# A gated DeltaNet layer whose convolution is done piece by piece behind each projection, with the scan traced closer together

## The chip, the cores and the metric

The kernel runs on one core of a Trainium2 chip. Its time is the device time of one execution in microseconds (us), from the first instruction to the last. Engines are named as in the profile: PE is the matrix engine (PEld its loading of weights), DVE the vector engine, ACT the scalar engine, POOL the GpSimd engine, SP the engine that issues most transfers. Every engine takes its instructions in the order of its own queue. An instruction waits on semaphores for what it needs of the other engines and of the DMA queues, and what stands behind it in its queue waits with it.

## What is computed

One step of a hybrid decoder with two layers, on 1,024 prompt tokens and 8 sequences of 8 new tokens (1,088 columns in all), with a width of 1,024. The first layer is a gated DeltaNet with 8 heads of 128, then a feed-forward layer; the second is a windowed attention mixture, then a feed-forward layer. The change touches the DeltaNet alone:

```python
proj = h @ w_in                                            # per head: q, k, v, gate of 128 columns each
xh = concat([conv_hist, proj[..., :A_CONV_DIM]], axis=1)    # 3 earlier rows ahead of the tokens
c = silu(causal_depthwise_conv(xh, conv_w))                 # 4 taps per column
q = l2_normalize(c_q) * A_DK ** -0.5; k = l2_normalize(c_k); v = c_v
...
def step(s, xs):                                            # one chunk of tokens of one head
    w_c, u_c, attn_c, q_c, k_c, ge_c = xs
    u = u_c - w_c @ s
    o = q_c @ s + attn_c @ u
    s = ge_c * s + k_c.T @ u
    return s, o
s_fin, o = lax.scan(step, s0, (w_mat, u_base, attn, q_dec, k_dec, g_end))
o = rms_norm(o, o_gain) * silu(gate)
```

Before the scan, each chunk needs the inverse of a triangular system of its decayed key products (`w_mat`, `u_base`).

## The kernel before

All values are float32; a product with weights is made as three passes of a split into a high and a low part (`h_hi`, `h_lo` and `w[0]`, `w[1]`), so one block of 128 output columns is 72 matmuls (L764).

A head goes through three stages, and three heads are worked on at a time. In round i of `gdn`, `gdn_scan` works on head i - 2, `gdn_prep` on head i - 1 and `gdn_dense` on head i; some gate projections fill the late rounds. `merge` traces the stages side by side: each yields the share of itself that it has just traced, and the one with the smallest sum goes next. From that tracing a scheduler makes the order of each engine's queue. So the numbers behind `yield` set how far apart the steps of a stage stand, in units of the others' work.

`gdn_dense` projects the three blocks (q, k, v) of a head, each in three chunks of tokens, 384, 352 and 352 wide (the last has 288 prompt and 64 new tokens). ACT copies a chunk from PSUM to the tile `xr` (L801, L803), which starts with 3 earlier rows. When all chunks of a block are there, `yc` is made from `xr`: ACT multiplies all 1,112 columns with the first tap (L809) and DVE adds the other three taps (L811). ACT's Silu follows (L813, L815), and the block goes to DRAM (L816). `xr` and `yc` have one buffer each; POOL clears the first 3 columns of the next `xr` at L795 and copies the last rows out at L805 and L806. Weights are loaded and split by `wtile`: ACT makes the high part (L142), POOL or DVE the low part (L145).

`gdn_prep` loads the head's q, k and v, transposes them on PE (L934), takes the keys' decay into `kdec` on DVE (L958) with their squares on ACT (L941), and makes the products of keys with keys and queries (L987). DVE builds the decay tile `aT` (L963), ACT its exponential (L965). `rq` is the queries' inverse norm (POOL's power at L1008 between DVE's L1007 and L1009). A row elimination on small blocks (L1020 to L1022, 15 steps) gives `dc`, from which DVE makes Dx (L1032), E (L1059) and its transpose F (L1048). NZ and NZ2 are two tiles that POOL clears (L1038) and ACT fills with parts of N (L1040, L1042); the first product of the inverse (L1054) takes NZ and F. NZ shares its buffer with the values and the queries.

`gdn_scan` goes through 8 chunks: p1 (L1166), r on DVE (L1168), p2 (L1173), u on ACT (L1175), p3 (L1178), the new state S on DVE (L1181), and the output from two products (L1185, L1187) with ACT's L1189 and DVE's L1190. The new tokens' step (`decode`, with POOL's `kqm` at L1121) is traced between the chunks. Behind the loop ACT squares the nine tiles of the output (L1203), POOL makes the factor (the norm chain, L1204 to L1208) and multiplies the output `vs` with it (L1211); PE transposes that (L1219) and ACT copies it out (L1225).

Of the kernel before, what the change touches and what calls it, by code (L numbers as in the profile page):

```python
# [22 lines left out]
P = 128  # L23
# [17 lines left out]
def tok(tt):  # L41
    return (tt * P, P) if tt < 8 else (SP, SD)


def merge(*threads):
    """Traces generators side by side: each yields the share of itself that it has just traced."""
    done = [[0.0, i, t] for i, t in enumerate(threads)]
    while done:
        done.sort()
        try:  # L50
            done[0][0] += next(done[0][2])
        except StopIteration:
            done.pop(0)


def staged(items, *stages):
    """Traces stage s of an item beside stage s + 1 of the item before; each takes the item and its last stage's result."""
# [8 lines left out]
def stream(*stages):  # L66
    """push(item) traces the first stage of an item, the second of the last item, and so on; None drains."""
# [12 lines left out]
class Net:  # L80
# [13 lines left out]
    def banks(self, **tags):  # L94
        """PSUM for the phase that follows: how many of the eight banks go around under each tag."""
# [6 lines left out]
    def weights(self, es, rb, wb, side=None):  # L102
        """Rotating [128, 1024] tiles for the enclosing phase: rb as they arrive, wb pairs of split weights."""
# [23 lines left out]
    def wtile(self, view, shape, gain=None, eng=None):  # L127
        """view: DRAM AP whose shape is `shape` ([128, a, b] or [128, n]); n <= 1024 columns."""
# [19 lines left out]
    def rstd(self, ss, p, n=D):  # L148
        """(ss / n + eps) ** -0.5 on a [p, c] tile."""
# [10 lines left out]
    def h_tiles(self):  # L160
        """High and low parts of a normed input, feature-major."""
        return tuple(self.hpool.tile([P, KD, T], F32R, tag=n, name=n) for n in ("h_hi", "h_lo"))

    def scale(self, tt, x, grow, xn=None):
        """Normed tokens x [p, 1024], times the gain if there is one."""
# [14 lines left out]
    def flipped(self, x, hi, lo, bank):  # L180
        """x [p, n * 128] feature-major, split, to hi and lo [128, n, p]."""
# [11 lines left out]
    def turn(self, tt, xn, h, bank):  # L193
        """xn feature-major, split, to its columns of h."""
# [10 lines left out]
    def residual(self, tt, y, xin, xout, grow, store=None):  # L205
        """x' = x + rms(y) * gain in place in y [p, 1024]; x' goes to xout in DRAM. A quarter of the columns is made without VectorE."""
# [16 lines left out]
    def fast_pool(self, es):  # L223
        """Space for the operands of fast products (see ffn_in), for the next chunk of the tokens; those that are free first lie together."""
# [12 lines left out]
    def stow(self, tt, x, grow):  # L237
        """Normed tokens x beside those of the other half that they go with."""
# [6 lines left out]
    def mate(self, tt, bank, tmp):  # L245
        """The seven moving operands of the fast product (see ffn_in) for tile tt of the second half and its mate of the first,
        one at a time; tmp() is [128, 1024]."""
# [1599 lines left out]
```

## Time and profile before

| | us |
|---|---|
| median of 3 runs | 3467.95 |
| lowest of the runs | 3462.15 |
| profiled execution: span, which is its own time | 3468.3 |
| PE busy in the span | 3104.6 (90%) |
| DVE busy | 2265.7 (65%) |
| ACT busy | 1556.7 (45%) |
| POOL busy | 1435.4 (41%) |

A row of the waits names the engine that waited, the line of the waiting instruction and, behind the arrow, the one that it waited for. In a timeline a row that ends with [idle before <- releaser] was preceded by idle time of that engine. The granted clock of PE (PEclk) is a share of its full speed.

### The profile page before, as it was taken

To read this page: it belongs to the slowest core of one execution; us is meant where nothing else is said; L and a number is where in the kernel's file an instruction comes from. 1 tells how busy PE (TensorE), PEld (TensorE's weight loads), DVE (VectorE), ACT (ScalarE), POOL (GpSimd) and SP (SyncE) were. 2 spreads that over 40 slices of the span, in tenths; PEclk is the share of its full clock that TensorE was granted. 3 is DMA by queue.
4 is the path that set the end of the run, shared out by engine and by line. 5 is a ranking of instruction groups with operands and counts; after the bars stand their busy time and mean duration, and the time that the engine had idled before them with its cause. 6 is when DMAs were issued, how large, how long until landed. Compare 5 with 4: busy or idle time off the path is not lost.

```text
span 3468.3 us, 53879 instructions
## 1 busy us (share of the span) xinstructions
PE 3104.6 (90%) x19768; PEld 2838.5 (82%) x19768; DVE 2265.7 (65%) x4705; ACT 1556.7 (45%) x3779; POOL 1435.4 (41%) x1368
## 2 busy tenths in 40 slices
PE   7899999999899999898899787978498999998996
PEld 7888888887799999776698787867276999997774
DVE  5677777625655555789767676767346655556888
ACT  5455554434433332533567676766134333334433
POOL 3333333343444443778421222221114344445877
PEclk8999999999999999999899998989789999999998
DMA  4223333344222221420531122213343122223213
GB/s 139 90 97 109 109 101 95 113 159 134 98 75 75 75 75 64 157 94 26 187 84 46 53 66 60 59 56 94 107 156 123 52 75 75 75 75 148 91 63 109
DMA packets 255588, 324.53 MB, mean 94 GB/s; under 512 B 33282, under 2 KB 204914, under 8 KB 255324
## 3 DMA queue, kind: packets, MB, share of 16 engines
q1 hardware_dynamic: 247324, 288.98, 26.1%
q0 software_dynamic: 7856, 31.56, 2.3%
q8 instruction: 156, 2.56, 0.3%
q14 instruction: 108, 0.88, 0.1%
q10 hardware_dynamic: 144, 0.56, 0.0%
HBM read 240.49 MB, written 80.55 MB: 93 GB/s over the span
## 4 chain that ended last, share of the span: by engine, by line
PE 56%; DVE 15%; DMA 8%; POOL 8%; ACT 6%; issue 4%; SPq 2%; POOLq 0%; DVEq 0%; ACTq 0%
PE mm L355 26%; PE mm L394 6%; PE mm L764 5%; PE mm L567 4%; DMA f<-fr 4%; PE mm L1344 2%; PE B L1054 2%; DVE og L1482 2%; SPq L1546 2%; ACT s L1435 2%; PE mm L1289 1%; DVE yc L811 1%; DVE qs L1355 1%; DVE wa L380 1%; PE A L987 1%
## 5 line engine op out<-in xcount | busy, mean ns | idle before, releaser
L394 PE MATMUL mm<-wa,ga 128*128 128x512 f32 x1872 | 474.8, 411 | 63.5 <-DVE wa L380 22.6
L394 PEld LDWEIGHTS mm<-wa,ga 128*128 128x128 f32 x1872 | 366.8, 198 | 165.2 <-DVE wa L380 32.8
L764 PE MATMUL mm<-h_hi,w 128*128 128x352 f32 (+1 forms) x1536 | 444.6, 348 | 10.5 <-ACT xr L801 8.2
L1344 PE MATMUL mm<-h_hi,w 128*128 128x352 f32 (+1 forms) x1152 | 374.3, 354 | 0.1
L764 PEld LDWEIGHTS mm<-h_hi,w 128*128 128x128 f32 x1536 | 283.5, 193 | 22.3 <-ACT xr L801 9.1
L323 POOL TENSOR_TENSOR wide<-wide,v 128x288 f32<-128x288 f32 (+1 forms) x176 | 162.3, 937 | 245.4 <-DVE v L322 245.4
L764 PE MATMUL mm<-h_lo,w 128*128 128x352 f32 (+1 forms) x768 | 260.0, 339 | 0.0
L304 DVE TENSOR_TENSOR s<-w,s 128x512 fp32r<-128x512 f32 x132 | 164.8, 1250 | 129.4 <-ACT s L303 129.2
L303 ACT ACTIVATE s<-t 128x512 fp32r<-128x512 f32 x176 | 111.0, 631 | 288.0 <-PE mm L355 275.0
L294 POOL TENSOR_TENSOR t<-w 128x512 f32<-128x512 f32 x88 | 114.6, 1304 | 299.0 <-issue 170.3
L1344 PEld LDWEIGHTS mm<-h_hi,w 128*128 128x128 f32 x1152 | 222.0, 197 | 0.6 <-PE mm L1344 0.3
L1435 ACT ACTIVATE s<-s,stat 128x128 f32<-128x128 f32 (+1 forms) x384 | 168.9, 441 | 106.4 <-DVE stat L1433 105.0
L1344 PE MATMUL mm<-h_lo,w 128*128 128x352 f32 (+1 forms) x576 | 194.3, 337 | 0.0
L567 PE MATMUL mm<-mw_hi,o_hl 128*128 128x512 f32 x544 | 176.4, 400 | 7.5 <-DVE o_hl L556 3.9
L1547 POOL TENSOR_TENSOR og<-og,f 128x512 f32<-128x512 f32 x42 | 53.7, 1278 | 285.1 <-DMA f<-fr 285.1
L1448 PE MATMUL tr<-ident,s 128*128 128x128 f32 x560 | 98.8, 285 | 72.1 <-DVE pl L1452 70.9
L145 POOL TENSOR_TENSOR w<-raw,w 128x1024 fp32r<-128x1024 f32 x38 | 100.6, 2649 | 146.4 <-ACT w L142 124.7
L304 DVE TENSOR_TENSOR s<-t,s 128x512 fp32r<-128x512 f32 x176 | 131.6, 749 | 39.7 <-ACT s L303 39.4
L355 PE MATMUL mm<-b0h,s 128*128 128x256 f32 (+1 forms) x704 | 144.8, 293 | 12.2 <-ACT s L303 9.6
L1452 DVE TENSOR_TENSOR pl<-tr,ph 128x256 fp32r<-128x256 f32 (+1 forms) x192 | 103.9, 544 | 78.1 <-ACT ph L1451 77.4
L811 DVE SCALAR_TENSOR_TENSOR yc<-xr,convw,yc 128x1112 f32<-128x1112 f32 x72 | 115.5, 1604 | 54.5 <-ACT yc L809 54.4
L764 PEld LDWEIGHTS mm<-h_lo,w 128*128 128x128 f32 x768 | 149.0, 194 | 1.9 <-issue 0.9
(477 smaller groups left out, 9559.6 us busy)
## 6 DMA issues: line engine op xcount, KB each, us to landing
w<-in_ffn_w_in_dram SPq DMA_DIRECT2D x88, 512.0 KB
gd<-wide POOLq DMA_DIRECT2D x22, 1088.0 KB, 4.9
graw<-gd SPq DMA_DIRECT2D x44, 544.0 KB
wraw<-in_ffn_w_out_dram SPq DMA_DIRECT2D x44, 512.0 KB
raw<-in_a_w_in_dram SPq DMA_DIRECT2D x32, 512.0 KB
qkv<-f SPq DMA_DIRECT2D x24, 544.0 KB
xo<-x SPq DMA_DIRECT2D x24, 512.0 KB
raw<-in_b_w_q_dram SPq DMA_DIRECT2D x24, 512.0 KB
```

Of the source, the lines that this page charges most:

```text
L294: op(t, x, y)
L303: nc.scalar.activation(out[j][:, 0], x, AF.Copy)
L304: nc.vector.tensor_sub(out[j][:, 1], x, out[j][:, 0])
L323: nc.gpsimd.tensor_tensor(out, out, v, op=ALU.mult)
L355: nc.tensor.matmul(ps[:, :HC[c][1]], u, v, start=z == 0, stop=z == 11)
L394: nc.tensor.matmul(ps, a, b, start=i == 0, stop=i == len(seq) - 1)
L567: nc.tensor.matmul(ps, a, b[:, k], start=k == 0 and i == 0, stop=k == KD - 1 and i == len(seq) - 1)
L764: nc.tensor.matmul(ps[:, :n], a[:, k, :], b[:, k, n0:n0 + n], start=i_ == 0, stop=i_ == 23)
L811: nc.vector.scalar_tensor_tensor(yc, xr[:, j:j + CW], w(j), yc, op0=ALU.mult, op1=ALU.add)
L1344: nc.tensor.matmul(ps[:, :n], a[:, k, :], b[:, k, n0:n0 + n], start=i == 0, stop=i == 23)
L1435: nc.scalar.activation(s[:, a, :n], s[:, a, :n], AF.Exp, bias=m, scale=-1.0, accum_out=stat[:, 1, a, b:b + 1])
L1452: nc.vector.tensor_sub(pl[:, :nk], pt[:, :nk], ph[:, :nk])
```

## The change

The convolution moves into the loop over the chunks of a block. As soon as a chunk has been copied to `xr`, ACT multiplies its columns with the first tap and DVE adds the other three; `yc` is taken at the start of the block. Per block that is 3 instructions on ACT where there was 1, and 9 on DVE where there were 3, of 384, 352 and 376 columns. In the scan, the square of chunk c - 1 is traced at step c, the last two behind the loop, and the yields of the scan's steps become smaller, those behind the norm larger. The docstrings are gone too, so lines shift: L811 becomes L810, L809 becomes L808, L813 L815, L958 L960, L987 L989, L1008 L1010, L1038 L1040, L1040 L1042, L1054 L1056, L1121 L1123, L1187 L1198, L1203 L1171, L1204 to L1208 L1211 to L1215, L1211 L1218 and L1219 L1226.

```diff
@@ gdn_dense
             nc.vector.tensor_copy(xd[:, :, 0:3], hist[:, tl].rearrange("p (b j) -> p b j", j=3))
+            yc = dp.tile([P, XW], F32, name="yc")[:, :CW]
+            w = lambda j: cv[:, j, tl:tl + 1]
             for y in self.gdn_proj(tl * P, h, w_in):
...
                     if n0 + n > SP:
                         nc.scalar.activation(xd[:, :, 3:], ps[:, a1 - n0:n].rearrange("p (b l) -> p b l", l=DL), AF.Copy)
+                        a1 = CW
+                    yy = yc[:, n0:a1]
+                    nc.scalar.activation(yy, xr[:, n0:a1], AF.Copy, scale=w(0))
+                    for j in range(1, 4):
+                        nc.vector.scalar_tensor_tensor(yy, xr[:, j + n0:j + a1], w(j), yy, op0=ALU.mult, op1=ALU.add)
                 yield 1 / 72
...
-            yc = dp.tile([P, XW], F32, name="yc")[:, :CW]
-            w = lambda j: cv[:, j, tl:tl + 1]
-            nc.scalar.activation(yc, xr[:, 0:CW], AF.Copy, scale=w(0))
-            for j in range(1, 4):
-                nc.vector.scalar_tensor_tensor(yc, xr[:, j:j + CW], w(j), yc, op0=ALU.mult, op1=ALU.add)
@@ gdn_scan
         dec = decode()
+        half = self.mhalf[:, :NT]
+        ss, f = small("ss_o"), small("f_o")
+        nc.gpsimd.memset(ss, 1.0)
+
+        def squares(c0, c1):
+            for c in range(c0, c1):
+                n = tok(c)[1]
+                j = rtile("junk")
+                nc.scalar.activation(j[:n], o[:n, c], AF.Square, accum_out=ss[:n, c:c + 1])
...
-                yield 0.02
+                yield 0.015
                 next(dec, None)
                 yield 0.01
...
-            yield 0.03
+            yield 0.02
...
-            yield 0.03
+            if c:
+                squares(c - 1, c)
+            yield 0.02
         nc.sync.dma_start(delta_p[hd], S)
         for _ in dec:
             pass
-        half = self.mhalf[:, :NT]
-        ss, f = small("ss_o"), small("f_o")
-        nc.gpsimd.memset(ss, 1.0)
-        for c in range(NT):
-            n = tok(c)[1]
-            j = rtile("junk")
-            nc.scalar.activation(j[:n], o[:n, c], AF.Square, accum_out=ss[:n, c:c + 1])
+        squares(7, 9)
...
-        yield 0.1
+        yield 0.15
         for s, n in parts:
             nc.gpsimd.tensor_tensor(o[:n, s], o[:n, s], bc(f, s, n), op=ALU.mult)
-        yield 0.1
+        yield 0.2
```

The queues have, in the whole program, 156 more rows on DVE (4,166 to 4,322; the listing counts some runs of like instructions as one row) and 70 more on ACT (2,540 to 2,610), 12 of them loads of ACT's function tables (23 to 35). Only the DeltaNet heads differ; from the mixer behind them to the end the order is the same on all engines. On PE, a steady head of before has 48 projections between the scan's last product (L1187) and the norm transposes (L1219), which stand directly ahead of the first product of the inverse (L1054). Now there are 78 (and five transposes of the values) ahead of the norm transposes (L1226), and six more between these and L1056. The scan's last product stands at 36.6 of a head's 62.8 units of the listing's PE work where it stood at 43.4.

Three places of a steady head follow, each before and now. On POOL, behind the scan of a steady head (ss_o and f_o are the norm chain, vs the output, kqm the new tokens' products of the next head), the queue was:

```order
L1038 MEMSET NZ 128x1024
L805 COPY last<-xr 128x3
L806 COPY last<-xr 128x24
L145 TENSOR_TENSOR w<-raw,w 128x1024
L976 MEMSET nc 64x16
L1204 TENSOR_TENSOR ss_o<-ss_o,rq 128x9
L1205 TENSOR_TENSOR ss_o<-ss_o,rq 128x9
L1206 TENSOR_SCALAR ss_o<-ss_o 128x9
L1207 TENSOR_TENSOR f_o<-ss_o,mhalf 128x9
L1208 TENSOR_TENSOR f_o<-f_o,rq 128x9
L1199 MEMSET ss_o 128x9
L1211 TENSOR_TENSOR vs<-vs,f_o 128x1024
```
and is now:

```order
L1010 TENSOR_TENSOR rq<-nq,mhalf 128x9
L953 MEMSET nq 128x9
L1211 TENSOR_TENSOR ss_o<-ss_o,rq 128x9
L1212 TENSOR_TENSOR ss_o<-ss_o,rq 128x9
L1213 TENSOR_SCALAR ss_o<-ss_o 128x9
L1214 TENSOR_TENSOR f_o<-ss_o,mhalf 128x9
L1215 TENSOR_TENSOR f_o<-f_o,rq 128x9
L1165 MEMSET ss_o 128x9
L1218 TENSOR_TENSOR vs<-vs,f_o 128x1024
L1218 TENSOR_TENSOR vs<-vs,f_o 64x128
L1123 TENSOR_TENSOR kqm<-qT_5871,Q_514 128x4x64
L1040 MEMSET NZ 128x1024
```
The clearing of NZ stood ahead of the weights' split and the norm chain; it stands behind the chain, the product and kqm, and the weights' split behind both. The power for rq is now directly ahead of the chain.

On ACT, at the end of the scan of a steady head (L1203 and L1171 are the squares, L801 and L803 the evacuations of a projection, u and t the scan's own), the queue was:

```order
L1203 ACTIVATE junk,ss_o<-vs 128x128
L1040 ACTIVATE NZ<-N 32x8x32 x4
L1175 ACTIVATE u<-C,bcol 128x128
L801 ACTIVATE xr<-mm 128x288
L803 ACTIVATE xr<-mm 128x8x8
L142 ACTIVATE w<-raw 128x1024
L1189 ACTIVATE t_6292<-C,gam 128x128
L809 ACTIVATE yc<-xr,convw 128x1112
L1203 ACTIVATE junk,ss_o<-vs 128x128
L1203 ACTIVATE junk,ss_o<-vs 64x128
```
and is now:

```order
L1171 ACTIVATE junk,ss_o<-vs 128x128
L1171 ACTIVATE junk,ss_o<-vs 64x128
L803 ACTIVATE xr<-mm 128x352
L808 ACTIVATE yc<-xr,convw 128x352
L1042 ACTIVATE NZ<-N 32x8x32 x4
L803 ACTIVATE xr<-mm 128x288
L805 ACTIVATE xr<-mm 128x8x8
L142 ACTIVATE w<-raw 128x1024
L808 ACTIVATE yc<-xr,convw 128x376
L967 ACT_TABLE_LOAD
L967 ACTIVATE aT<-aT 128x512
L815 ACT_TABLE_LOAD
```
The copies into NZ stood ahead of the scan's last u and t; they stand behind the last squares, and two evacuations of xr, the weights' copy and the first tap of the 376 columns stand behind them.

On DVE, at the start of the next head's preparation (kdec is needed by the key products on PE), the queue was:

```order
L811 SCALAR_TENSOR_TENSOR yc<-xr,convw,yc 128x1112
L958 TENSOR_TENSOR kdec<-A,kds 128x512
L811 SCALAR_TENSOR_TENSOR yc<-xr,convw,yc 128x1112
L1183 COPY S<-C 128x128
L811 SCALAR_TENSOR_TENSOR yc<-xr,convw,yc 128x1112
L1192 COPY vs<-C 128x128
L796 COPY xr<-hist 128x8x3
L958 TENSOR_TENSOR kdec<-A,kds 128x512
L1168 SCALAR_TENSOR_TENSOR r<-C,ngam,vs 128x128
```
and is now:

```order
L810 SCALAR_TENSOR_TENSOR yc<-xr,convw,yc 128x352 x3
L810 SCALAR_TENSOR_TENSOR yc<-xr,convw,yc 128x376 x2
L960 TENSOR_TENSOR kdec<-A,kds 128x512
L810 SCALAR_TENSOR_TENSOR yc<-xr,convw,yc 128x376
L1194 COPY S<-C 128x128
L796 COPY xr<-hist 128x8x3
L1203 COPY vs<-C 128x128
L1179 SCALAR_TENSOR_TENSOR r<-C,ngam,vs 128x128
L960 TENSOR_TENSOR kdec<-A,kds 128x512
```
The second kdec had three passes of 1,112 columns around and ahead of it; it has one of 376 between itself and the first kdec, and shorter passes ahead of that.

## Rows read from the trace of the kernel before

**Rows 1.** Windows, all and six steady heads: length, busy PE, PEld, DVE, ACT, POOL.

```profile
44.00:787.00 743.00, 680.24 (x4482) 629.43 (x4482) 465.92 (x1262) 354.41 (x1046) 254.15 (x312) 0.96 0.35 111
...
152.00:628.00 476.00, 432.82 (x2907) 398.42 (x2907) 332.42 (x918) 240.50 (x744) 166.92 (x211) 0.96 0.33 102
```

**Rows 2.** PE's waits, 44 to 787 us: total us, times, longest.

```profile
PE C L1219 <- POOL vs L1211: 26.0, 7, 4.1
PE A L987 <- DVE kdec L958: 11.5, 6, 2.0
PE mm L764 <- ACT xr L801: 8.2, 3, 4.1
PE A L934 <- DMA vT<-qkv: 5.5, 7, 1.4
```

**Rows 3.** The timeline around L1219, one steady head: start, duration, engine, line.

```profile
359.61 0.39 PE L1187 MATMUL C<-S,qT 128*128 128x128 f32 x2
...
362.58 0.20 ACT L1203 ACTIVATION_READ_ACCUMULATOR junk<-vs 64x1 f32 x1
...
364.55 1.05 POOL L1204 TENSOR_TENSOR ss_o<-ss_o,rq 128x9 f32<-128x9 f32 x1
...
370.22 2.30 POOL L1211 TENSOR_TENSOR vs<-vs,f_o 128x1024 f32<-128x1024 f32 x2
...
372.17 1.54 PE L1219 MATMUL C<-ident,vs 128*128 128x128 f32 x6 [4.12 <-POOL vs L1211]
...
372.18 0.43 DVE L1048 STREAM_TRANSPOSE F<-E 128x256 f32<-128x256 f32 x1
...
372.48 0.72 POOL L1121 TENSOR_TENSOR kqm<-qT,Q 128x256 f32<-128x256 f32 x1
```

**Rows 4.** The timeline around L987 of the same head.

```profile
313.88 3.48 POOL L145 TENSOR_TENSOR w<-raw,w 128x1024 fp32r<-128x1024 f32 x1 [3.08 <-ACT w L142]
...
315.23 3.31 DVE L811 SCALAR_TENSOR_TENSOR yc<-xr,convw,yc 128x1112 f32<-128x1112 f32 x1
...
319.81 0.49 PE L987 MATMUL A<-kT 128*128 128x128 f32 x2 [2.00 <-DVE kdec L958]
```

**Rows 5.** The windows view behind both stalls; PEclk stands after the engines.

```profile
320.00:322.00 2.00, 2.00 (x12) 2.00 (x12) 1.11 (x6) 0.75 (x2) 1.82 (x3) 0.60 1.16 339
322.00:324.00 2.00, 2.00 (x11) 2.00 (x10) 1.00 (x4) 0.00 (x0) 0.82 (x3) 0.55 0.60 238
372.00:374.00 2.00, 1.83 (x9) 1.83 (x10) 2.00 (x6) 0.68 (x1) 1.24 (x4) 0.50 0.85 300
```

**Rows 6.** Single lines L811, L1204, L1008: ns min/median/max.

```profile
L811 DVE SCALAR_TENSOR_TENSOR yc<-xr,convw,yc x72: 1356/1374/3395, 48.4 to 633.5; 128x1112 f32<-128x1112 f32 x72
...
L1204 POOL TENSOR_TENSOR ss_o<-ss_o,rq x8: 208/1047/1050, 204.6 to 755.1; 128x9 f32<-128x9 f32 x8
...
L1008 POOL TENSOR_TENSOR rq<-nq,mhalf x8: 1794/1795/2973, 115.9 to 663.9; 128x9 f32<-128x9 f32 x8
```

**Rows 7.** The lines by form, 44 to 700 us: busy us, mean ns.

```profile
L1168 DVE SCALAR_TENSOR_TENSOR r<-C,ngam,vs 128x128 f32<-128x128 f32 x49 | 16.9, 344 | 1.8 <-PE C L1166 0.6
...
L1032 DVE TENSOR_TENSOR Dx<-dc,sel 128x1024 f32<-128x1024 f32 x8 | 9.7, 1215 | 0.1
...
L809 ACT ACTIVATE yc<-xr,convw 128x1112 f32<-128x1112 f32 x24 | 29.7, 1237 | 0.1
...
L142 ACT ACTIVATE w<-raw 128x1024 fp32r<-128x1024 f32 x27 | 28.8, 1066 | 0.1
...
L1203 ACT ACTIVATE junk<-vs 128x128 f32<-128x128 f32 x56 | 17.1, 315 | 9.2 <-DVE vs L1190 9.2
...
L1040 ACT ACTIVATE NZ<-N 32x256 f32<-32x256 f32 x32 | 13.2, 414 | 2.4 <-POOL NZ L1038 2.1
...
L813 ACT ACT_TABLE_LOAD x9 | 11.5, 1283 | 0.2
...
L1038 POOL MEMSET NZ<- 128x1024 f32 x16 | 15.3, 955 | 109.5 <-PE A L934 57.9 <-PE A L987 51.6
```

## The prediction

> **What bounds the kernel now.** I read first the busy time by stage [rows 1]. The part that the change touches, the DeltaNet heads at 44 to 787 us, takes 743 us, of which PE is busy 680.2; six steady heads fill 152 to 628, 79.3 us each. From 787 on the order of every engine is the same as before, so 2,681 us stay as they are. PE is the bound with 91%, and only its 62.8 idle us and the stretches at a lower clock can be won. DVE (465.9) and ACT (354.4) have room on average. The span of the profiled execution is 3468.3 us, and nothing around it is counted; the median of the runs is 3467.95, so a difference against the one is a difference against the other.
>
> Second, PE's waits in that part [rows 2]. Three lines carry 45.7 of the 62.8 us: the norm transposes (L1219) behind POOL's product `vs` (7 times, 26.0), the key products (L987) behind DVE's `kdec` (6 times, 11.5), and projections behind the evacuation of `xr` (3 times, 8.2, all in the first heads). Call the first stall A, the second B.
>
> Third, the timeline of one steady head around A [rows 3]. The scan's last product (L1187) ends at 360.00. PE has 48 projections, done at 368.05 (372.17 less the 4.12 us that the L1219 row gives as idle), so 0.17 us each. The squares end at 362.78; POOL's norm chain starts at 364.55, its product ends at 372.52, and PE moves when the large part of it is there, at 372.17. F, which the first product of the inverse needs (L1054), is transposed at 372.18, so it is late too: should the norm chain come earlier, F is next.
>
> Fourth, the same for B [rows 4]: a convolution pass of DVE takes 3.31 us where its median is 1.37 [rows 6], while POOL splits weights (3.48 us); by the order of DVE the second part of `kdec` is queued behind three such passes, and PE idles 2.00 us. Fifth, the clock [rows 5]: granted 0.50 in the 2 us after A, a loss of 1.0 us, and 0.60 and 0.55 in the 4 us after B, 0.8 + 0.9 = 1.7 us. [...]
>
> **Part 1: the convolution in pieces.** Each of 24 blocks has 3 passes of 1,112 columns on DVE; now it has 9 of 384, 352 and 376. From 128 columns at 344 ns (L1168) and 1,112 at the median of 1,374 ns, a column costs (1374 - 344) / 984 = 1.047 ns and an instruction 210 ns [rows 6, 7]; that gives 0.61, 0.58 and 0.60 us for the three sizes. Six more instructions per block cost 1.26 us, 24 blocks 30 us. On ACT, L809 (1,237 ns) and L1203 (128 columns, 315 ns) give 0.94 ns a column and 0.2 us per instruction: two more per block, 24 blocks, 9 us. The order has 12 more table loads for Silu and Exp (35 for 23), at 1.28 us 15 us [rows 7]. All that lies on DVE and ACT, which stay at 496 and 379 of 743 us; beside PE it is hidden. If the cover is gone, which is the case only where PE waits for DVE, it costs up to 3.8 us a head (30 / 8).
>
> [...]
>
> What the pieces bring: only the last piece is left when a block's projections end. So `kdec` has one short piece ahead of it where two or three long passes stood, and stall B goes, with its clock: -2.0 - 1.7 = -3.7 per steady head (bounds 0 and -3.7; I take all, since the DVE rows ahead shrink by over 2 us). What is late next there: the key's own DMA and squares, which the waits show only in small. In the first heads `xr` comes free sooner: -8.2 once.
>
> **Part 2: the squares.** ACT's order before has them along the scan already, one by one, so the edit itself moves nothing: 0. The chain still starts with the last two.
>
> **Part 3: other yields.** The scan stands earlier in a head's projections: before the norm transposes PE has 78 projections behind it instead of 48, and 84 before the first product of the inverse. That is 84 x 0.17 = 14.5 us, with 12 transposes (six took 1.54 us at a lowered clock; I take 0.15 each) 16.3 us of work. The norm chain ends 12.5 us after the scan (360.00 to 372.52): it is covered by 78 projections (13.5 us), and stall A at the norm transposes goes.
>
> But another wait takes its place. POOL now clears NZ behind the norm chain, no longer ahead of it. ACT queues the copies into NZ, two evacuations of `xr`, the weights' copy and the last piece's first product behind that; DVE queues the last passes, the last two rows, Dx, E and F behind this product. From the scan's end: squares 2.8, norm chain 8.0 (364.55 to 372.52), 10.8; kqm 0.72 and the clearing 0.96, 12.5; four copies of 0.41, 14.1; evacuations of 288 and 64 columns about 0.6 (an estimate, two ACT instructions of the size of L1203), weights 1.07, the piece 0.55 (0.2 + 376 columns at 0.94 ns), 16.3; on DVE three pieces of 0.60, Dx 1.2, E and F 0.43 each, and about 12 small ones at 0.31 (an estimate, from L1168's 0.34 for 128 columns), 7.6, so 23.9 [rows 3, 7]; POOL's weight split now falls into this and stretches a pass by 1.9 as in [rows 4]: F at 25.8. PE has 16.3 us of work, so it waits 9.5 where it waited 4.1: +5.4. The evacuation of `xr`, which frees the bank of a projection, is in the same queue and only takes a share of the same wait. With nothing stretched (POOL's chain at 4.9 us, from four small ones at L1204's least, 0.21, a power at L1008's 1.80 and the product's 2.30 [rows 3, 6], and no 1.9) F comes at 20.9 and A grows by 0.5. Bounds +0.5 and +5.4; I take +4, nearer to the stretched end, because DVE is as full there as in the rows.
>
> Two small terms. POOL's power for `rq` (L1008, median 1.80 us, at most 2.97) [rows 6] now comes while the scan's last steps run, and DVE's next instruction, which waits for it, stands ahead of the new state of chunk 6: between 0 and 2.97 us, I take +1.5, nearer to the median, since the scan has other work of PE behind it. The value transposes stand behind the scan's last product, and their DMA (5.5 us, 7 times) has landed: -0.8 a head (0 to -0.8).
>
> **Sum.** A steady head: +4.0 - 3.7 + 1.5 - 0.8 = +1.0, six of them +6. First heads -8.2. In the seventh head with both a scan and an inverse (628 to 718 us) no block is convolved, so no piece stands before F, and A goes there: 26.0 / 7 = -3.7. Together 6 - 8.2 - 3.7 = -6: 3468 - 6 = **3462 us**, own range 3445 to 3480 (the steady sum is off by up to 3 us a head).
>
> **Rivals.** (1) Everything works as written: A, B and the `xr` waits vanish and nothing replaces them. -45.7, and clock 7 x 1.0 + 6 x 1.7 = 17.2: -63, 3405 us. For it: the norm chain and `kdec` do have the room; against it, F at 372.18 was already as late as A, and NZ's clearing is moved behind the chain.
> (2) The slower side, one mechanism: NZ's clearing behind the norm chain holds ACT, and through it DVE. A head then pays the full 5.4 at A, a second low-clock stretch because the wait is split between the projection's bank and F (1.5, an estimate between the 1.0 and the 1.7 of [rows 5]), `kdec` stays late since DVE runs behind (B stays, 0), 1.5 for `rq`, -0.8: +7.6, six heads +46, first heads -8.2: +38, 3506 us. It decides from the point where F comes more than 16.3 + 4.1 + 3.7 = 24 us after the scan's last product, for then A grows by more than B gives. With the rq wait at 2.97 in every head and two more scan steps stopped as long, 7.4 more in six heads, 44 us, it would pass 3537.
> (3) The scheduler had undone the old yields as it had the squares, and the stretches only change places: 3468. Against it: 78 projections in place of 48.
>
> **How the numbers follow.** Forecast 0.50, rival 1 0.27, rival 2 0.19, rival 3 0.04. 2% is 69 us (3398.6 and 3537.3), about what a measurement of this kernel can tell from no change. Rival 1 with the remaining idle time in it (62.8 + 17.2 = 80) would pass 3398.6: 0.05 of its 0.27. Of rival 2, 0.03 lies past 3537. So faster 0.05, slower 0.03, same 0.92. The range runs from just below rival 1 to just above rival 2, 3398 to 3510: what is left out is the far end of each, under 2 in 10.
>
> **What would show it.** Right: no wait of L1226 for `vs`, a new wait of L1056 (for F) or of a projection for `xr` of 5 to 10 us in six heads, NZ's copies on ACT waiting for POOL, no wait of L989 over 1 us. Wrong: PE's idle time in this part under 25 us (rival 1), or over 100 us and heads of 86 us (rival 2); a changed time after the last head.

## The result and the profile after

The changed kernel takes 3491.91 us (median of 4 runs, 3486.41 to 3496.33) against 3468.93 us for the kernel before on the same chip: ratio 1.0073, 95% interval 1.0058 to 1.0089. The ratio is of the fast runs alone, and one of the four executions of the kernel before, at 5602.14 us, is not among them. It is slower by 0.7%, where a gain of 6 us was forecast. Its profiled execution has a span of 3494.6 us.

The three stages of the DeltaNet part, bounded by the first p2 of a head's scan and the start of the next layer's mixer, in the kernel before and in the changed one (columns as in [rows 1], the mean granted clock stands after the engines):

```profile
44.00:152.60 108.60, 96.90 (x608) 91.94 (x608) 61.00 (x157) 51.59 (x122) 23.39 (x35) 0.95 0.36 110
152.60:628.00 475.40, 432.22 (x2903) 397.84 (x2902) 332.42 (x918) 239.90 (x743) 166.92 (x211) 0.96 0.33 102
628.00:791.20 163.20, 151.81 (x978) 140.04 (x976) 72.50 (x187) 64.34 (x184) 65.36 (x68) 0.98 0.44 140
```

```profile
44.00:155.50 111.50, 96.66 (x601) 92.22 (x599) 65.69 (x193) 55.63 (x135) 24.65 (x38) 0.92 0.36 107
155.50:655.30 499.80, 436.24 (x2898) 393.83 (x2898) 343.05 (x1026) 268.73 (x788) 141.17 (x209) 0.95 0.32 98
655.30:817.50 162.20, 152.47 (x979) 139.31 (x977) 66.04 (x188) 63.93 (x184) 63.23 (x68) 0.98 0.42 135
```

The first heads take 2.9 us more (108.60 to 111.50), the six steady heads 24.4 more (475.40 to 499.80, 4.07 a head), the last stretch 1.0 less: 26.3 together, which is the difference of the spans (3494.6 - 3468.3). So the loss is made in the steady heads. There PE's busy time rises by 4.0 us for the same work, and its idle time from 43.2 to 63.6 us. The waits of those six heads, before and after (engine, line, what it waited for, total us, times, longest):

```profile
PE C L1219 <- POOL vs L1211: 24.7, 6, 4.1
PE A L987 <- DVE kdec L958: 11.5, 6, 2.0
PE A L934 <- DMA vT<-qkv: 5.2, 6, 1.4
```

```profile
PE B L1056 <- DVE F L1050: 46.7, 6, 9.3
PE C L1184 <- DVE r L1179: 5.4, 5, 1.1
PE A L936 <- DMA vT<-qkv: 3.1, 5, 1.1
```

Stall A at the norm transposes (the first row, part of [rows 2]) is gone, and so is stall B at the key products. In A's place stands one wait: the first product of the inverse (L1056) for F, 46.7 us in six heads. The timeline of the head that answers to [rows 3]:

```profile
360.77 0.39 PE L1198 MATMUL C<-S,qT 128*128 128x128 f32 x2
...
362.43 0.21 DVE L1023 TENSOR_TENSOR row<-row,nc 128x63 f32<-128x63 f32 x1
...
362.72 0.25 POOL L1211 TENSOR_TENSOR ss_o<-ss_o,rq 128x9 f32<-128x9 f32 x1 [6.33 <-ACT junk L1171]
...
363.02 0.43 SPq L956 DMA_DIRECT2D aT<-gcd  x1
...
363.68 1.80 POOL L1214 TENSOR_TENSOR f_o<-ss_o,mhalf 128x9 f32<-128x9 f32 x1
...
364.46 0.25 DVE L1024 TENSOR_TENSOR dc<-dc,row 128x81 f32<-128x81 f32 x1
...
365.88 2.65 POOL L1218 TENSOR_TENSOR vs<-vs,f_o 128x1024 f32<-128x1024 f32 x2
...
366.33 1.94 DVE L1024 TENSOR_TENSOR dc<-dc,row 128x90 f32<-128x90 f32 x1
...
370.14 1.70 ACT L1042 ACTIVATE NZ<-N 32x256 f32<-32x256 f32 x4 [5.03 <-POOL NZ L1040]
...
373.38 0.59 ACT L808 ACTIVATE yc<-xr,convw 128x376 f32<-128x376 f32 x1
...
373.56 2.39 POOL L145 TENSOR_TENSOR w<-raw,w 128x1024 fp32r<-128x1024 f32 x1 [0.88 <-ACT w L142]
...
374.06 2.04 DVE L965 SCALAR_TENSOR_TENSOR aT<-aT,gc,U 128x128 f32<-128x128 f32 x1 [3.87 <-DMA aT<-gcd]
...
384.27 0.45 DVE L1050 STREAM_TRANSPOSE F<-E 128x256 f32<-128x256 f32 x1
...
384.86 2.05 PE L1056 MATMUL B<-F,NZ 128*128 128x128 f32 x8 [8.01 <-DVE F L1050]
```

The scan's last product ends at 361.16. PE works until 376.85 (384.86 less the idle 8.01), 15.7 us, and F comes at 384.72, 23.6 us after the scan. Two things are late at 374 us, both at once: the last piece of the convolution has its first tap at 373.97, at the end of the chain NZ, copies, evacuation, weights, tap; and DVE stands idle from 370.2, for 3.87 us, at an instruction of the next head, aT (L965), whose data were asked for at 363.02 and are there at 374.06; the rest of the elimination stands behind it in the queue. Then comes a full queue: in the row at 362.43 the elimination of `gdn_prep` stands at a width of 63 columns; it goes in steps of 9 columns to 135, so nine steps lie behind the scan. In the kernel before, where the scan ends at 360.00, the step at 117 columns is under way and two are left (126 and 135):

```profile
359.85 0.28 DVE L1021 TENSOR_TENSOR row<-row,nc 128x117 f32<-128x117 f32 x1
...
361.33 2.22 DVE L1022 TENSOR_TENSOR dc<-dc,row 128x126 f32<-128x126 f32 x1
...
369.66 0.42 DVE L1059 TENSOR_TENSOR E<-dc,par 128x256 f32<-128x256 f32 x1
...
370.67 1.59 DVE L963 SCALAR_TENSOR_TENSOR aT<-aT,gc,U 128x128 f32<-128x128 f32 x1 [0.59 <-DMA aT<-gcd]
```

There the load of aT is waited for too, but behind E (369.66), and for 0.59 us.

The clock behind the wait for F in that head, and one more window behind stall A of the kernel before, to be read beside [rows 5]:

```profile
384.00:386.00 2.00, 1.14 (x5) 1.17 (x6) 1.97 (x7) 1.18 (x2) 0.00 (x0) 0.50 0.00 0
386.00:388.00 2.00, 2.00 (x12) 2.00 (x11) 0.79 (x2) 0.28 (x1) 0.00 (x0) 0.50 0.00 0
388.00:390.00 2.00, 2.00 (x11) 2.00 (x11) 0.00 (x0) 1.04 (x3) 0.00 (x0) 0.50 0.34 45
390.00:392.00 2.00, 2.00 (x16) 2.00 (x16) 0.50 (x2) 0.00 (x0) 0.00 (x0) 0.81 0.61 242
```

```profile
374.00:376.00 2.00, 2.00 (x15) 2.00 (x15) 1.64 (x8) 0.67 (x3) 0.00 (x0) 0.75 0.08 30
```

After 8 us without work PE is granted 0.50 in three windows and 0.81 in the next: 0.57 + 1.0 + 1.0 + 0.38 = 2.95 us lost. Behind stall A the loss went on into the window that [rows 5] does not show, 0.9 + 0.5 = 1.4 us, and behind stall B it was 1.7. One head is not enough to judge this, so here are all six. The loss is PE's busy time times what is missing of the granted clock, added up over windows of 0.5 us behind each wait:

| us lost to the clock | wait of PE | behind the six waits | sum |
|---|---|---|---|
| before, stall A | 4.1 each | 2.9, 1.7, 1.4, 1.7, 2.7, 1.5 | 12.0 |
| before, stall B | 2.0 (the first 1.5) | 0, 1.7, 1.7, 0, 1.7, 1.7 | 6.8 |
| changed, wait for F | 6.6, 6.9, 8.0, 8.0, 7.8, 9.3 | 2.5, 1.9, 2.9, 1.6, 2.8, 2.7 | 14.5 |

So the low clock costs 4.3 us less in the six heads than before, and its cost does not follow the length of the wait: it is 1.4 to 2.9 us behind six equal waits of 4.1 us, and 2.9 and 1.6 behind two of 8.0. (The mean clock of the whole stretch falls from 0.96 to 0.95 all the same, since it also counts the time in which PE is idle: it is 0.55 from 380.0 to 384.8 us, where PE has no work.) PE's busy time rises by 4.0 us although less is lost to the clock, so some 8 us more of it lie at the full clock. What stretches it there was not traced.

### The profile page after: what moved, and what is told of

It is laid out like the page before. It is cut to its first block, busy times and chain, and to the rows that moved or that the text cites. A ratio compares the mean times of both kernels' runs of the same rounds, so it can differ in the third digit from the quotient of the medians.

```text
span 3494.6 us, 54064 instructions
## 1 busy us (share of the span) xinstructions
PE 3105.5 (89%) x19768; PEld 2831.0 (81%) x19768; DVE 2279.8 (65%) x4849; ACT 1591.1 (46%) x3839; POOL 1411.1 (40%) x1368
## 4 chain that ended last, share of the span: by engine, by line
PE 55%; DVE 16%; DMA 9%; POOL 7%; ACT 6%; issue 4%; SPq 2%; POOLq 0%; DVEq 0%; ACTq 0%
PE mm L355 26%; PE mm L394 6%; PE mm L764 5%; PE mm L567 4%; DMA f<-fr 4%; PE mm L1351 3%; DMA aT<-gcd 2%; PE B L1056 2%; SPq L1553 2%; DVE og L1489 2%; ACT s L1442 1%; PE mm L1296 1%; DVE qs L1362 1%; DVE yc L810 1%; DVE wa L380 1%
## 5 line engine op out<-in xcount | busy, mean ns | idle before, releaser
L810 DVE SCALAR_TENSOR_TENSOR yc<-xr,convw,yc 128x352 f32<-128x352 f32 (+2 forms) x216 | 138.3, 641 | 41.8 <-ACT yc L808 39.4
L145 POOL TENSOR_TENSOR w<-raw,w 128x1024 fp32r<-128x1024 f32 x38 | 93.5, 2461 | 141.5 <-ACT w L142 120.0
```

The source lines that it names most:

```text
L810: nc.vector.scalar_tensor_tensor(yy, xr[:, j + n0:j + a1], w(j), yy, op0=ALU.mult, op1=ALU.add)
```

## The experiments

Each ratio is against the kernel before on the same chip, with its 95% interval. Of each, one shortened edit is shown.

**The two halves apart.** `conv_only` is the kernel before with the new `gdn_dense`, `scan_only` the kernel before with the new `gdn_scan`.

```diff
conv_only: gdn_dense of after, gdn_scan of before
scan_only: gdn_dense of before, gdn_scan of after
```

> Before with the convolution in pieces alone; squares and yields as before. Theory (the closer scan costs, the pieces gain): the wait for kdec at the key products (11.5 us in six heads) goes with its slow stretch, the norm transposes still wait for vs about 4 us a head: -3.7 x 6 = -22, about 3447 us, and no wait of the inverse's first product for F over 2 us. Rival (the pieces themselves cost, by their fixed time on DVE and ACT's table loads): F is late here too, 3475 to 3490 us.

> Before with the squares along the scan and the new yields alone; the convolution in whole passes. Theory (the closer scan costs): F behind three long passes, so the wait of the inverse's first product for F is as long as in the changed kernel, 8 us a head, and kdec still waits 2 us: 3495 to 3510 us. Rival (the pieces cost): about 3468 us, as before, or lower.

Measured: 3471.74 us, 1.0009 (0.9997 to 1.0021), and 3489.0 us, 1.0048 (1.0033 to 1.0063); heads of 79.3 and 82.6 us. Both lie outside the ranges of theory and rival, `scan_only` on the side that its theory had. The pieces alone change nothing, the scan alone costs some 17 us. PE's wait for F is 36.1 us in `scan_only`. In `conv_only` the profile puts the waits of the inverse's first product down to F twice and to POOL's norm chain five times:

```profile
PE B L1056 <- POOL ss_o L1208: 12.1, 5, 2.4
PE B L1056 <- DVE F L1050: 9.6, 2, 7.1
```

```profile
PE B L1054 <- DVE F L1048: 36.1, 6, 6.1
```

That product takes F and NZ and nothing of the norm chain, and in all seven heads it starts 0.14 or 0.15 us after the end of F's transpose; POOL's instruction only ended at about the same time. One such head of `c_hold2`, a run that follows below:

```profile
363.80 0.43 DVE L1051 STREAM_TRANSPOSE F<-E 128x256 f32<-128x256 f32 x1
...
364.03 0.21 POOL L1209 TENSOR_SCALAR ss_o<-ss_o 128x9 f32<-128x9 f32 x1
...
364.37 2.02 PE L1057 MATMUL B<-F,NZ 128*128 128x128 f32 x16 [2.41 <-POOL ss_o L1209]
```

F ends at 364.23 there, POOL's instruction at 364.24. So these waits are counted as F's from here on, and the wait for F in `conv_only` is 21.7 us.

In both runs DVE waits 31.2 us for aT (9.6 before), so the load is late with either half.

**The two late things, one at a time.** `a_aT3` gives aT a third buffer, so that its load can start a head earlier; `a_NZ` gives the second half of NZ a buffer of its own and takes NZ from kT's, so that it is cleared without waiting for the norm chain. Both make room by sharing small tiles.

```diff
-        N, aT = slot("N"), slot("aT", bufs=2)
+        N, aT = slot("N"), slot("aT", bufs=3)
```

```diff
-        NZ, NZ2 = slot("NZ", "qT"), slot("NZ2", "kT")
+        NZ, NZ2 = slot("NZ", "kT"), wk.tile([P, 8, P], F32, name="NZ2")
```

> The changed kernel with three buffers for the decay tile aT in place of two, so that its load is issued a head earlier (room is made by letting two small tiles share a buffer and junk have one; nothing is left out). Theory (the load of aT, on which DVE idles 3.9 us a head ahead of the last pieces, is what ends last before F): F comes 4 to 4.5 us earlier in six heads, -24 to -27, about 3466 us, the wait for F falls from 7.8 to about 3.5 us a head. Rival (the prediction's chain: NZ's clearing, ACT, DVE): the load is beside it, no change, 3488 to 3496 us.

> The changed kernel with NZ in the keys' buffer and NZ2 in one of its own, so that both are cleared well ahead of the norm chain and ACT never waits for that (same room-making as a_aT3; nothing is left out). Theory (the load of aT ends last): F stays where it is, 3488 to 3496 us, the wait for F about 7.8 us a head still, ACT's wait for NZ (5 us a head) gone. Rival (the prediction's chain): the last piece comes 5 us earlier, F with it, 5 x 6 = -30, about 3462 us.

Measured: 3518.14 us, 1.0134 (1.0119 to 1.0149), and 3512.36 us, 1.0121 (1.0103 to 1.0139). Both missed: `a_aT3` lies 52 us above its theory and `a_NZ` 16 us above the upper end of its theory's range, and both lie above their rivals' too. In `a_aT3` DVE comes to its aT instructions 4 us after the load was issued, where it came 7 us after it in the changed kernel:

```profile
376.37 0.37 SPq L956 DMA_DIRECT2D aT<-gcd  x1
...
388.66 0.35 DVE L965 SCALAR_TENSOR_TENSOR aT<-aT,gc,U 128x128 f32<-128x128 f32 x1 [8.32 <-DMA aT<-gcd]
```

A wait of 8.32 us, where it was 3.87; over the part DVE waits 56.8 us for aT. In `a_NZ` ACT hardly waits for NZ any more (1.1 us in the part for 32.7) and DVE waits 56.8 us for aT there too: in the head of the other rows it stands idle until 387.50, for 7.90 us, where the last tap was done at 384.73. So NZ's clearing, the prediction's cause, is not what ended F's wait there. Whether it is the third buffer that moved the reader in `a_aT3` is not shown: both runs share the edits that make room, and DVE's wait for aT is as long in `a_NZ`, where aT has two buffers.

**Holding the reader instead.** `a_hold` lets DVE take up the next head's aT only behind F, `a_hold2` behind the transposed X of the end of the inverse; the load stays where it is. `a_hold2_NZ` adds the NZ edit.

```diff
+                with self.tc.issue_after(st["F"]) if "F" in st else ExitStack():
                     nc.vector.scalar_tensor_tensor(aT[:n, e, :n], ...
...
-        turned(E, X)
+        st["F"] = turned(E, X).ins
```

> The changed kernel, with DVE's nine instructions on the next head's decay tile aT ordered behind the transpose F of the head before; nothing else is edited. Theory (DVE's wait for the load of aT, 3.9 us a head, and the nine instructions ahead of F make F late): F comes about 6 us earlier in six heads, the wait for F falls from 7.8 to about 2 us a head, 3491 - 35 = 3455 us (3447 to 3465). Rival (the prediction's chain from NZ's clearing ends last): the last piece still waits for it, F moves by under 2 us, 3480 to 3492 us.

> As a_hold, but DVE's instructions on aT are ordered behind the last transpose of the inverse (E from X), some 7 us later. Theory: the second wait, of the inverse's later products for what DVE makes behind aT, goes as well: 0 to 12 us below a_hold. Rival (aT is then late for the key products' masks): above a_hold by 6 us or more.

> a_hold2 and a_NZ together: aT held back, NZ and NZ2 cleared early in buffers of their own. Theory (once aT is out of the way, NZ's clearing is next in line): the rest of the wait for F, about 2 us a head, goes: 8 to 15 us below a_hold2, with no wait for F over 1 us. Rival (NZ is beside the path): as a_hold2, within 4 us.

Measured: 3483.2 us, 1.0039 (1.0026 to 1.0053); 3486.38 us, 1.0049 (1.0031 to 1.0068); 3487.15 us, 1.0047 (1.0029 to 1.0066). `a_hold` lies in its rival's range and not in its theory's, and the further gains expected of the other two did not come. The wait for aT is gone (one of 5.3 us is left in the part), yet only 8 to 12 us of the 25 come back, and with NZ free as well nothing more. F is still waited for, 35.5 us in `a_hold2`, and now DVE has work nearly all the way. The stretch from the end of the scan to F in `a_hold2`, and the rows on DVE that are stretched in it, and F:

```profile
357.50:377.60 20.10, 14.59 (x91) 13.90 (x89) 18.37 (x52) 8.64 (x20) 10.00 (x15) 0.97 0.45 126
```

```profile
362.71 1.95 DVE L1025 TENSOR_TENSOR dc<-dc,row 128x90 f32<-128x90 f32 x1
...
370.41 2.35 DVE L810 SCALAR_TENSOR_TENSOR yc<-xr,convw,yc 128x376 f32<-128x376 f32 x1 [0.87 <-ACT yc L808]
...
377.11 0.44 DVE L1051 STREAM_TRANSPOSE F<-E 128x256 f32<-128x256 f32 x1
```

DVE is busy for 18.37 of 20.10 us and idle once for longer, 0.87 us at the last piece; PE has 14.59 us of work there. So behind aT and NZ stands DVE's own work. Some 4 us of it are the stretch of DVE's instructions beside two long ones of POOL (last section), an estimate from these rows and the 0.25 and 0.60 us that they take alone; no run moved POOL's work away.

**The pieces without the closer scan, with the reader held.** `c_hold2` is `conv_only` with the edit of `a_hold2`; `b_hold2` and `s_hold2` put that edit into the kernel before and into `scan_only`.

> conv_only (before, with the convolution in pieces) with DVE's instructions on aT held as in a_hold2. Theory: its waits of the inverse for F and behind it (32 us in six heads) are the load of aT as well; 15 to 25 us below conv_only, 3447 to 3457 us, so the pieces by themselves gain once DVE doesn't wait for that load. Rival (the pieces' own time on DVE): as conv_only, 3468 to 3474 us.

> Before, with DVE's instructions on the next head's aT held behind the last transpose of the inverse; nothing else. Theory: before waits only 9.6 us in all for that load, mostly beside PE's work, so 3462 to 3472 us. Rival (the gain of c_hold2 is the hold's and not the pieces'): about 3442 us, as c_hold2.

> scan_only (before, with the closer scan, the squares along it and the longer yields behind it) with aT held as in b_hold2. Theory (the closer scan costs by itself, since DVE's elimination is left behind it): still 10 to 20 us over before, 3478 to 3490 us, the wait for F 4 to 6 us a head. Rival (the closer scan costs only through the load of aT): 3455 to 3470 us.

Measured: `c_hold2` 3442.27 us, 0.9933 (0.9908 to 0.9958); `b_hold2` 3463.69, 0.9975 (0.9958 to 0.9992); `s_hold2` 3480.55, 1.0028 (1.0015 to 1.0041). By the ratios, in us against the kernel before at 3469:

| | conv as before, scan as before | pieces, scan as before | conv as before, scan closer | both |
|---|---|---|---|---|
| aT as it is | 0 | +3 | +17 | +25 |
| aT's reader held | -9 | -23 | +10 | +17 |

`b_hold2` and `s_hold2` came as expected; `c_hold2` gained 5 us more than its range. The closer scan costs in every pair, 17 to 40 us. The pieces gain 14 with the old scan and the reader held, and seem to lose 7 or 8 beside the closer scan, where the intervals, about 5 us either way, touch or overlap. `c_hold2`, with its heads of about 75 us, is faster than both kernels of the case. Its wait for F is 16.2 us, where `a_hold2` has 35.5:

```profile
PE B L1057 <- POOL ss_o L1209: 12.1, 5, 2.4
...
PE B L1057 <- DVE F L1051: 4.1, 2, 2.3
```

That is 19 us of the 54.8 by which the profiled executions of the two differ. PE's busy time in the DeltaNet part is 31 us less (688.4 to 657.1), and the clock granted from 44 to 787 us is 0.97 for 0.96; where the 31 us come from is open.

**Which part of the closer scan.** `u_steps` puts the yields within the scan's steps back, `u_tail` those behind it, `u_sq` the squares; the rest stays as changed. `u_hold_steps` is `u_steps` with the reader held, `u_sq_hold2` `u_sq` with it.

```diff
u_steps, and the like twice more
-                yield 0.015
+                yield 0.02
u_tail
-        yield 0.15
+        yield 0.1
...
-        yield 0.2
+        yield 0.1
u_sq
-            if c:
-                squares(c - 1, c)
...
-        squares(7, 9)
+        squares(0, 9)
```

> The changed kernel with the yields of the scan's steps as before (0.02, 0.03, 0.03); pieces, squares along the scan and the longer yields behind the norm stay. Theory (tracing the steps closer is what costs: the scan ends earlier among the projections, and DVE's elimination, which takes its time whatever PE does, is left behind it): as conv_only, 3468 to 3476 us, no wait for F over 2.5 us but for single ones. Rival (the yields behind the norm cost): 3485 to 3495 us, as the changed kernel.

> The changed kernel with the yields behind the norm as before (0.1 and 0.1); the steps stay closer. Theory (the steps cost): the norm transposes are early again and wait for vs, but F still comes last; 3488 to 3500 us. Rival (the yields behind the norm cost): 3468 to 3476 us.

> The changed kernel with the squares traced behind the loop again, all nine; everything else as changed. Theory (the squares are beside the path, and ACT's queue took them between the steps anyway): 3488 to 3496 us. Rival (squares in the scan's steps hold up u or t on ACT): 5 to 15 us less than the changed kernel.

> u_steps with DVE's instructions on aT held behind the last transpose of the inverse, as in c_hold2: the pieces, the squares and the yields behind the norm of the change, without its closer steps. Theory: as c_hold2, 3436 to 3448 us, under both kernels. Rival (the gain of c_hold2 needs the old yields behind the norm or the squares at the end): above 3455 us.

> u_sq (the changed kernel with the squares behind the loop) with aT held. Theory (u_sq was slow because DVE waited 54.6 us for aT in all where the changed kernel waits 30.8, not because of the squares): 3480 to 3490 us, as a_hold2. Rival (the squares at the end cost by themselves): over 3505 us.

Measured: `u_steps` 3488.68 us, 1.0048 (1.0031 to 1.0065), a miss; `u_tail` 3490.31, 1.0055 (1.0034 to 1.0076); `u_sq` 3518.83, 1.014 (1.0125 to 1.0155), a miss; `u_hold_steps` 3464.22, 0.9978 (0.9965 to 0.9991), a miss; `u_sq_hold2` 3484.41, 1.0043 (1.0027 to 1.0058). The squares move nothing by themselves: with the reader held the two orders are within their intervals (1.0043, 1.0049), and what `u_sq` lost is DVE's 54.6 us of waiting for aT. The old steps do bring the wait for F down, from 49.1 to 27.5 us (the first two rows), but with the new tail another one comes up:

```profile
PE B L1056 <- DVE F L1050: 20.7, 6, 7.9
PE B L1056 <- POOL ss_o L1213: 6.9, 1, 6.9
PE C L1177 <- DMA kT<-qkv: 13.9, 6, 3.0
```

The next scan's first product waits for its kT, six times. By the code that tile shares its buffer with `ot`, which a longer tail frees later; that this is what makes the load late was not tried. `u_tail` has its time in the expected range, but not for the expected reason: the wait for F is down to 3.4 us, and PE stops ahead of it, at the norm transposes, for ACT's copy of their output:

```profile
PE C L1226 <- ACT ot L1232: 35.8, 6, 8.2
```

In the head that answers to the other rows that copy stands on ACT behind the exponential of aT, which waits for DVE's aT, 18.9 us in the part. With the reader held the old steps alone give back 25 of the 40 us between `a_hold2` and `c_hold2` (1.0049, 0.9978, 0.9933); the rest is the tail's or the squares', which moved nothing beside the closer steps.

**Is it DVE's work?** `a_hold2_tap` and `c_hold2_tap` leave out two of DVE's three taps of the convolution, 144 of 216 instructions, some 86 us of DVE.

```diff
-                    for j in range(1, 4):
+                    for j in range(1, 2):
```

> a_hold2 with one of the three DVE passes of each piece, so the convolution has two taps in place of four: this leaves out work of DVE and nothing of PE, ACT or POOL. Theory (with aT out of the way DVE's own work between the scan's end and F is the bound): F 3 to 4 us earlier, 18 to 25 us under a_hold2, 3461 to 3468 us, the wait for F under 2.5 us a head. Rival (F waits for NZ's chain over ACT): under 5 us of change, 3481 to 3490 us.

> The convolution in pieces with the old scan and the held load's consumer, and two of three DVE taps left out (24 blocks x 6 instructions of 0.6 us, some 86 us less of DVE in all; the output then lacks two taps of the convolution). Theory that DVE's work behind the scan is the bound only where the scan stands closer: without the closer scan PE hardly waits for F (4.1 us in the part), so taking the taps out gives at most what PE still waits for POOL's sums and F here, 0 to 16 us: 3426 to 3442. Rival, that DVE's sum over a head is the bound whatever the scan's place: the taps give as much as they did with the closer scan, 49 us: about 3393. If the first holds, the same taps are worth three times as much with the closer scan as without it.

Measured: 3437.53 us, 0.9912 (0.9894 to 0.9929), and 3431.2 us, 0.9888 (0.987 to 0.9906). Against their partners the taps are worth 48 us with the closer scan (1.0049 to 0.9912; the expectation was 18 to 25, a miss in size) and 16 without it (0.9933 to 0.9888). With the taps left out the two scans are 8 us apart, where they were 40. In `a_hold2_tap` the scan's last product ends at 341.56 in the head below, and F comes 9.9 us after it, where it came 20.0 us after it in `a_hold2` (357.53 to 377.55):

```profile
351.01 0.45 DVE L1051 STREAM_TRANSPOSE F<-E 128x256 f32<-128x256 f32 x1
...
351.60 0.57 PE L1057 MATMUL B<-F,NZ 128*128 128x128 f32 x3 [1.99 <-ACT xr L803]
```

The wait put down to `xr` is F's again, 0.14 us after its end. In all, F is waited for 15.7 us instead of 35.5, in heads of about 75 us for 82. In `c_hold2_tap` it is 16.2 us, as in `c_hold2`. So with the closer scan the amount of DVE's work sets how long PE waits for F, and with the old scan it does not. This is not the whole of the 48 us: the wait for F is 20 of them, and PE's busy time in the part is 23 us less (688.4 to 665.7), at a granted clock of 0.98 for 0.96 (44 to 787 us); where these come from is open. Nor is it DVE's time alone that moved: PE has 8.0 us of work between the scan and F in `a_hold2_tap` and 14.9 in `a_hold2`, so the order has shifted with it. And the copies into NZ end at 351.10 there, only 0.4 us ahead of F, so the prediction's chain is now as late as DVE's.

## Why the prediction was wrong

Three steps failed. A steady head was forecast at +1.0 us and came at +4.07, 18 of the 32 us between -6 and +26; there the step "stall B goes, with its clock" counted 1.7 us of clock as won in each head and took PE's busy time to change by nothing else (+0.7 us a head measured). The first heads were forecast at -8.2 and came at +2.9, 11 us; there nothing was taken to stand behind the waits for `xr`. The seventh head was to give 3.7 and gave 1.0. And in the path that makes stall A longer the step failed that puts NZ's clearing, ACT and the last piece ahead of F: F came late behind the load of aT and DVE's own queue.

**The size of stall A: right, with another cause in it.** Forecast were 9.5 us of waiting where it was 4.1, taken as +4.0. Measured: (46.7 - 24.7) / 6 = +3.7 a head. PE's work before F was sized at 16.3 us and took 15.7, F at 25.8 us after the scan and came at 23.6. But the chain was not what the prediction drew. The norm chain took 5.8 us (362.72 to 368.53), not 8.0; in place of that stood a wait of 3.87 us for the load of aT, which no step of the prediction names, and the elimination. Of this it counted the "last two rows" behind the last tap; nine steps were behind the scan, and the wait for aT left those from 99 columns on, and aT's own instructions, for the time behind 374 us. Both are rows of DVE between the scan and F. Two errors of opposite sign made a good number, and that is luck. (A slip: 84 x 0.17 is 14.3 and not 14.5 us.)

**B: right.** The wait for `kdec` went, -1.9 a head for -2.0.

**The small terms.** The wait for `r`, that is for POOL's power `rq`, is 5.4 / 6 = 0.9 a head for 1.5 taken; the value transposes gain 0.35 for 0.8; 1.1 a head came from waits that were not forecast (Y, `xr`, S and some smaller).

**The clock and PE's busy time: the largest miss of the steady sum.** Stall B's loss of 1.7 us was taken as won in each head, and A's as unchanged. By the table above B lost 6.8 us in six heads, since two of its waits cost nothing, and F's waits lose 2.5 more than A's did: the clock gave back 0.7 us a head. PE's busy time rose none the less, from 432.2 to 436.2 us, +0.7 a head where -1.7 was forecast. That is 2.4 of the 3.1 us by which a head (+4.07 for +1.0) came out too low: 1.0 of clock, and 1.4 of busy time at the full clock, whose cause no run shows. The rest is A -0.3, `rq` -0.6, the transposes +0.45 and the small waits +1.1, and 0.1 for `kdec`.

**The first heads: -8.2 forecast, +2.9 measured.** The three waits for `xr` did go, down to one of 1.1 us, but the path behind them was set by the load of kT. It is issued at 90.31 us in the kernel before and at 90.33 now, and the transposes start at 94.30 and 94.36: PE only waited in another place, 7.6 us where it had waited 2.1. What holds the issue there was not traced.

```profile
90.31 0.33 SPq L948 DMA_DIRECT2D kT<-qkv  x1
...
94.30 1.23 PE L934 MATMUL A<-ident,kT 128*128 128x128 f32 x8 [2.10 <-DMA kT<-qkv]
```

```profile
90.33 0.33 SPq L950 DMA_DIRECT2D kT<-qkv  x1
...
94.36 1.97 PE L936 MATMUL A<-ident,kT 128*128 128x128 f32 x8 [7.62 <-DMA kT<-qkv]
```

This is the step that the prediction took without asking "what is late next", 11 us of the 32 between -6 and +26. **The seventh head** gave 1.0 for 3.7. The forecast took the mean of seven waits, 26.0 / 7, but six of them make up 24.7, so the seventh had only 1.3 to give, and 1.2 are still there.

**The pieces on DVE.** An instruction of 352 to 384 columns has a median of 604 ns, as the 0.58 to 0.61 us of the prediction; DVE's busy time rose by 8.9 us and not by 30 (the three stretches sum to 465.92 and 474.78). The long passes had been stretched (72 took 115.5 us, 1.60 us each) and the short ones are less often (means of 0.62 to 0.66 us), so that the convolution rose by some 23 us, an estimate from these means; other rows gave time back, aT's from 28.8 to 23.3. The prediction's 210 ns for an instruction and 1.047 ns for a column, its estimates from rows of 128 and 1,112 columns, come to 604 ns for 376 columns, so they hold at these sizes. What those extra instructions cost was put at "hidden beside PE"; the prediction gave a price, 3.8 us a head, for the case in which PE waits for DVE. That case came: the tap runs show that DVE's work counts there. That beside the closer scan the pieces seem to lose 7 to 8 us, where they gain with the old one and the reader held, agrees with it.

**The rivals.** Rival 2 had the side right. Its point was F at 24 us, and F came at 23.6, but its mechanism, NZ behind the norm chain, is not what decides: with NZ free and aT held nothing was won (`a_hold2_NZ`). What decides, by the pairs and the tap runs, is that a scan traced closer together takes PE's projections out of the scan and leaves DVE's elimination for the time behind it, where PE has only 15.7 us of work for 18 to 20 of DVE. How much of the time each step of this makes is shown in part only: PE's busy time moves with it, and that was not explained.

Open is how much of the load of aT, some 11 us from issue to use in both kernels (359.80 to 370.67, 363.02 to 374.06), is the transfer itself; no run changed its form.

## What to carry to other kernels

Tracing one thread closer together does not only move its own wait: it leaves the other threads' work for later, so count, on every engine, the rows between the new place of the wait and the instruction that ends it, those of other stages and their loads too. Where a wait is taken away, ask in the same sentence what else arrives at that moment; here a load issued at a fixed time took over the whole gain in the first heads. Price the low clock behind a wait from all its occurrences and not from one: here six equal waits of 4.1 us cost between 1.4 and 2.9 us. And where a wait names an unlikely releaser, look at what ended just before it: here waits put down to POOL's norm chain and to ACT's `xr` were F's.

## What the runs showed of the hardware

In two places of the changed kernel's timeline a DVE instruction that runs beside one of POOL's lasts until about the end of that: `dc` took 1.94 us instead of about 0.25 (366.33 to 368.27) beside POOL's product (365.88 to 368.53), and aT 2.04 instead of 0.34 (374.06 to 376.10) beside POOL's split of weights (373.56 to 375.95); the ends lie within 0.3 us of each other. Beside POOL's power (363.68 to 365.48) it was not so: there the elimination's rows of 81 columns took 0.24 and 0.25 us, and in the other five steady heads 0.24 each. The length of these meetings follows POOL's instruction and not the size of DVE's: in `a_hold2` 90 columns took 1.95 us beside the product of 2.65 and 376 columns 2.35 us beside the split of 2.39, where they take 0.25 and 0.60 alone. What couples the two engines there is not shown.
